# Three-block sequence model on one core: the first modulation tiles issued from POOL's queue, row tiles split over two pools, output scaled in pairs

## The chip, the cores and the metric

The kernel runs on one core of a Trainium2 chip. The metric is the device time of one execution in microseconds; three runs of a kernel are taken and their median is compared.

## What is computed

Three transformer-like blocks are applied to x of 256 tokens by 2048 channels, in float32. Cut to what matters here:

```python
c_act = jax.nn.silu(c)                                # c: 1 x 2048
mod = c_act @ w_ada[l] + b_ada[l]                     # 2048 x 12288
shift1, scale1, gate1, shift2, scale2, gate2 = jnp.split(mod, 6, axis=-1)
h = rms_norm(x, norm1) * (1.0 + scale1[:, None]) + shift1[:, None]
proj = h @ w_in                                       # block 1: gated delta rule, stick-breaking
...
x = second_block(x, mem_2, ...)                       # km, vm = projections of normed mem
return third_block(x, ..., final_norm_g_3)            # ends with rms_norm(x, final gain)
```

## The kernel before

x lies transposed: 16 tiles `x_k` of 128 channels by 256 tokens. Weights arrive as float32 tiles of 128x2048 (1 MiB each). Most matmuls split both operands: ScalarE writes a rounded high half (`whi`, `a` from line 390) and DVE the rest (`wlo` line 291, `a` line 391), and TensorE adds hi·hi, hi·lo and lo·hi. Every engine and queue runs its instructions in one fixed order, which a scheduler sets when the program is built; an instruction waits for semaphores, and what stands behind it waits too.

The head of the program is `block1` (line 516 on):

- `ada_start` loads c, applies SiLU and spreads it over the partitions (`csilu`). `ada_queue` then holds the 96 modulation tiles of w_ada, of which the first 32 give shift1 and scale1.
- `ada_tile` (line 489) loads one such tile, and DVE multiplies it by `csilu` and sums each row into a column of `mod` (line 496, 128x2048), then adds b_ada (line 498). The first 32 take their buffer from the pool `early`, tag "ada", three buffers; later ones share the weight pool's tag "wraw", three buffers (`WRAW`). All loads are issued by SyncE (SP).
- `load_mem` and `memory_kv` scale two tiles of mem into 16 `mh` tiles (line 951) and make four `km` tiles (matmuls at line 970, norm from line 972 on) and four `vm` tiles (line 990) for block 2; `load_x` is called before the fourth km, and modulation tiles are called for in between. The results go to DRAM (`kv_spill`).
- `project_rows` (line 593) takes 16 row tiles `wrow` of w_in's rows, one per k, from `early`, tag "rows", three buffers. For each k DVE scales x_k (line 611), ScalarE adds the shift (line 612), x_k is split, half of the row tile is split (`whi`, `wlo`), and 8 plain and 24 split matmuls run (line 623; the trace shows a plain one twice).
- The heads of block 1 follow, and then the other blocks, with weights from "wraw".

The tail: the last down-projection adds into `x[n]` for n = 0 to 15, squares go into `ssq`, `rstd_rows` makes the token scale, and `store_x` (line 467) writes x·gain·rstd with 16 DVE operations (line 472) and 16 stores of 128 KB (line 475).

Of the kernel before, what the change touches and what calls it, by code (L numbers as in the profile page):

```python
# [9 lines left out]
F32 = mybir.dt.float32  # L10
# [3 lines left out]
AF = mybir.ActivationFunctionType  # L14
ALU = mybir.AluOpType
# [3 lines left out]
P = 128  # L19
T = 256  # L20
D = 2048
KT = D // P
NFF = 5632 // P
GFF = 11
WRAW = 3
ADA_LATE = 6
NSPLIT = 8
X_AT = 3
SPILL_K = 7
# [175 lines left out]
class Core:  # L205
# [259 lines left out]
            self.square_acc(self.ssq, self.x[k], k == 0)  # L465

    def store_x(self, final=True):
        r = self.rstd_rows(self.ssq) if final else None
        for k in range(KT):
            if final:  # L470
                o = self.gt()
                self.nc.vector.scalar_tensor_tensor(o, self.x[k], self.vec("final", k), r, op0=ALU.mult, op1=ALU.mult)
            else:
                o = self.x[k]
            self.nc.sync.dma_start(self.out[:, k], o)

    def ada_start(self):
        nc, ins = self.nc, self.ins
        self.cs = self.adap.tile([P, D], F32, name="csilu")
        row = self.early.tile([P, D], F32, name="crow", tag="ada", bufs=3)[0:1]  # L480
        nc.sync.dma_start(row, ins["c"])
        for j in range(4):
            p = self.psum(False)
            nc.tensor.matmul(p, self.ones[0:1], row[:, j * 512:j * 512 + 512], start=True, stop=True)
            nc.scalar.activation(self.cs[:, j * 512:j * 512 + 512], p, AF.Silu)
        self.mod = self.const.tile([P, 96], F32, name="mod")
        self.ada_queue = [j + 16 * (1 - b) for j in range(16) for b in range(2)] + list(range(32, 96))

    def ada_tile(self, n):
        nc = self.nc  # L490
        if n < 32:
            raw = self.early.tile([P, 2048], F32, name=self.uid("ada"), tag="ada", bufs=3)
        else:
            raw = self.wp.tile([P, 2048], F32, name=self.uid("ada"), tag="wraw", bufs=WRAW)
        nc.sync.dma_start(raw, self.ins["w_ada"][n])
        nc.vector.scalar_tensor_tensor(raw, raw, 1.0, self.cs, op0=ALU.mult, op1=ALU.mult, accum_out=self.mod[:, n:n + 1])  # L496
        if n < 32:
            nc.vector.tensor_add(self.mod[:, n:n + 1], self.mod[:, n:n + 1], self.vec("b_ada", n))
        elif n % 16 == 15:
            k = VCOL["b_ada"]  # L500
            nc.vector.tensor_add(self.mod[:, n - 15:n + 1], self.mod[:, n - 15:n + 1], self.vecs[:, k + n - 15:k + n + 1])
# [14 lines left out]
    def block1(self):  # L516
        nc, ins = self.nc, self.ins
        with self.tc.tile_pool(name="ada", bufs=1) as self.adap:
# [11 lines left out]
            with self.tc.tile_pool(name="b1", bufs=1) as bp:  # L530
                self.bp = bp
                mixed = self.block1_mix()
                self.ada_some(96, 16 + ADA_LATE)
                h2 = []
# [58 lines left out]
    def project_rows(self, rstd, spills):  # L593
        nc = self.nc
        accs = [self.psum(width=512) for _ in range(2)]
        for lane in "SAB":
            with self.on(lane):
                accs += [self.psum(False) for _ in range(2)]
        self.hs = []
        for k in range(KT):  # L600
            while len(self.ada_queue) > 64 + 2 * max(0, KT - 2 - k):
                self.ada_some(1)
            raw = self.early.tile([P, 2048], F32, name=self.uid("wrow"), tag="rows", bufs=3)
            nc.sync.dma_start(raw, self.ins["w1_rows"][k])
            if k == SPILL_K:
                for dst, src in spills:
                    nc.sync.dma_start(dst, src)
            g = self.tp.tile([P, 1], F32, name=self.uid("gk"), tag="gk")
            nc.vector.scalar_tensor_tensor(g, self.mod[:, 16 + k:17 + k], 1.0, self.vec("norm1", k), op0=ALU.add, op1=ALU.mult)
            h = self.x[k]  # L610
            nc.vector.scalar_tensor_tensor(h, h, g, rstd, op0=ALU.mult, op1=ALU.mult)
            nc.scalar.activation(h, h, AF.Identity, bias=self.mod[:, k:k + 1])
            self.hs.append(self.split(h))
            parts = [self.split_weights(raw, a, min(1024, NSPLIT * P - a)) for a in range(0, NSPLIT * P, 1024)]
            for j in range(len(ROWS)):
                cols = slice(j * P, j * P + P)
                if j < NSPLIT:
                    whi, wlo = (t[:, j % 8 * P:j % 8 * P + P] for t in parts[j // 8])
                    pairs = [(whi, m) for m in self.hs[k][:2]] + [(wlo, self.hs[k][0])]
                else:  # L620
                    pairs = [(raw[:, cols], h)]
                for i, (w, m) in enumerate(pairs):
                    nc.tensor.matmul(accs[j // 2][:, j % 2 * T:j % 2 * T + T], w, m,  # L623
                                     start=(k == 0 and j % 2 == 0 and i == 0),
                                     stop=(k == KT - 1 and j % 2 == 1 and i == len(pairs) - 1))
        self.stash = {}
        for j, key in enumerate(ROWS):
            if j % 2 == 0:
                pair = self.act_halves("row")
            t = pair[j % 2]  # L630
            src = accs[j // 2][:, j % 2 * T:j % 2 * T + T]
            nc.gpsimd.memset(t[:, 0:3], 0.0)
            if j % 2:
                nc.vector.tensor_copy(t[:, 3:T + 3], src)
            else:
                nc.scalar.copy(t[:, 3:T + 3], src)
            self.stash[key] = t
# [35 lines left out]
    def proj(self, name, j):  # L673
        self.ada_some(1, 16 + ADA_LATE)
        return self.ftile(self.ins[name][j], self.hs)
# [182 lines left out]
    def sb_head(self, h, ob):  # L858
        nc, ins, c = self.nc, self.ins, self.c
        if h % 2 == 0:  # L860
            accs = self.ttile([ins["w1_sv"][h // 2, j] for j in range(2)], self.hs)
            self.sv = []
            for t in range(2):
                v = self.tmp("sv", (P, T), bufs=4)
                nc.scalar.copy(v, accs[t][:, :T])
                self.sv.append(v)
            self.ada_some(2, 16 + ADA_LATE)
        accq = self.proj("w1_sq", h)
# [65 lines left out]
    def memory_kv(self, load_x=None):  # L934
        nc, ins = self.nc, self.ins
# [7 lines left out]

        ssq = self.gt()
        for half, raw in enumerate(self.mem):
            pool, tag, bufs = (self.early, "rows", 3) if load_x else (self.wp, "wraw", WRAW)
            sq = pool.tile([P, 2048], F32, name=self.uid("msq"), tag=tag, bufs=bufs)
            nc.scalar.activation(sq, raw, AF.Square)
            for j in range(8):
                h = held()  # L950
                nc.vector.tensor_scalar(h, raw[:, j * T:j * T + T], self.vec("mem_g", half * 8 + j), None, op0=ALU.mult)
                hs.append(h)
            for w in (1024, 512):
                nc.vector.tensor_add(sq[:, :w], sq[:, :w], sq[:, w:2 * w])
            if half:
                nc.vector.tensor_add(ssq, ssq, sq[:, :T])
                nc.vector.tensor_add(ssq, ssq, sq[:, T:2 * T])
            else:
                nc.vector.tensor_add(ssq, sq[:, :T], sq[:, T:2 * T])
# [3 lines left out]
        for h in range(4):  # L963
# [15 lines left out]
            r = self.gt()  # L979
# [533 lines left out]
    def block3(self):  # L1513
        nc, ins = self.nc, self.ins
        hs = [self.split(self.x[k], self.vec("norm1_3", k)) for k in range(KT)]
        rstd, rcol = self.rstd_rows(self.ssq), self.rstd_cols(self.ssq)
        mixed = [None] * 16
        with self.tc.tile_pool(name="b3", bufs=1) as bp:
            cp = bp
            self.block3_mix(bp, hs, rstd, rcol, mixed)  # L1520
            self.ssq = self.new_ssq()
            for n in range(KT):
                self.wadd(self.x[n], self.wtile(ins["w3_out"][n], mixed))
                self.square_acc(self.ssq, self.x[n], n == 0)
        hs = [self.split(self.x[k], self.vec("norm2_3", k)) for k in range(KT)]
        rstd = self.rstd_rows(self.ssq)
        self.ssq = self.new_ssq()
        for g in range(NFF // GFF):
            a = []
            for f in range(g * GFF, (g + 1) * GFF):  # L1530
                acc = self.wtile(ins["w3_gate"][f], hs)
                gt = self.wmul(self.gt(), acc, rstd)
                nc.scalar.activation(gt, gt, AF.Silu)
                acc = self.wtile(ins["w3_up"][f], hs)
                nc.vector.tensor_mul(gt, gt, rstd)
                nc.vector.tensor_mul(gt, gt, self.wsum(self.gt(), acc))
                a.append(self.split(gt))
            for n in range(KT):
                self.wadd(self.x[n], self.wtile(ins["w3_down"][g, n], a))
                if g == NFF // GFF - 1:  # L1540
                    self.square_acc(self.ssq, self.x[n], n == 0)

    def block3_mix(self, bp, hs, rstd, rcol, mixed):
        nc, ins, tp = self.nc, self.ins, self.tp
# [152 lines left out]
```

## Time and profile before

| what | value |
|---|---|
| median of three runs | 3597.47 us (3594.34 to 3597.59) |
| the profiled execution's own time | 3601.28 us |
| span of its profile | 3599.5 us |
| TensorE busy | 3514.4 us, 98% |
| DVE busy | 2662.4 us, 74% |
| ScalarE busy | 1814.2 us, 50% |
| mean DMA rate over the span | 195 GB/s |

Busy times are of one profiled execution, and times in the rows are microseconds from the start of its span. Idle time is named with what ended it. TensorE's weight loads are counted apart and overlap its matmuls.

### The profile page before, as it was taken

How to read it: one execution, taken by the hardware profiler on the slowest of the kernel's cores; microseconds unless marked ns; L12 is line 12 of the kernel's file. 1: busy time of each engine (PE TensorE's matmuls, PEld its weight loads, DVE VectorE, ACT ScalarE, POOL GpSimd, SP SyncE). 2: the span in 40 equal slices, each digit the busy share in tenths (PEclk: the TensorE clock that was granted, in tenths of full speed). 3: DMA queues.
4: the chain of work that ended last, by engine and by line, in shares of the span. 5: the costliest groups of instructions: out<-in, count | busy, mean ns of one | idle time of the engine just before them, and what ended most of it. 6: DMA issues, size and time to landing. Idle time of an engine off the chain costs nothing.

```text
span 3599.5 us, 59008 instructions
## 1 busy us (share of the span) xinstructions
PE 3514.4 (98%) x22656; PEld 3144.6 (87%) x22656; DVE 2662.4 (74%) x5500; ACT 1814.2 (50%) x3138; POOL 61.6 (2%) x190
## 2 busy tenths in 40 slices
PE   8889999999999999999999999999999999999998
PEld 6889998999999998888888888889888888888887
DVE  7788988776767668877878867778776666666666
ACT  4156665544545455555555545554444544444444
POOL 0000000000000000000000000000000000000000
PEclk9989999999999999999999999999999999999999
DMA  8965777656666557332234336574445545555554
GB/s 337 351 237 200 263 266 265 225 208 219 222 206 231 188 181 239 133 125 107 103 115 138 125 117 213 188 253 170 172 168 185 187 176 202 176 198 180 195 184 144
DMA packets 128011, 700.99 MB, mean 195 GB/s; under 512 B 14449, under 2 KB 39537, under 8 KB 58865
## 3 DMA queue, kind: packets, MB, share of 16 engines
q1 hardware_dynamic: 127730, 697.22, 55.0%
q8 instruction: 179, 2.93, 0.3%
q14 instruction: 102, 0.84, 0.1%
HBM read 686.94 MB, written 10.22 MB: 194 GB/s over the span
## 4 chain that ended last, share of the span: by engine, by line
PE 86%; DVE 8%; ACT 3%; DMA 1%; issue 1%; SPq 0%; ACTq 0%; DVEq 0%
PE acc L335 36%; PE acc L339 18%; PE acc L309 12%; PE acc L313 6%; DVE wlo L291 2%; DVE ada L496 2%; PE acc L1349 1%; ACT whi L290 1%; PE acc L1358 1%; PE acc L1359 1%; PE acc L623 1%; PE acc L990 1%; PE acc L374 1%; DMA ada<-in_w_ada 1%; PE acc L369 1%
## 5 line engine op out<-in xcount | busy, mean ns | idle before, releaser
L290 ACT CAST whi<-wraw 128x1024 fp32r<-128x1024 f32 x1118 | 1096.1, 982 | 1199.0 <-PE acc L335 706.9
L291 DVE TENSOR_TENSOR wlo<-wraw,whi 128x1024 fp32r<-128x1024 f32 x1118 | 1272.7, 1140 | 514.5 <-ACT whi L290 412.4
L335 PE MATMUL acc<-a,whi 128*128 128x512 f32 x5888 | 1535.6, 396 | 6.7 <-ACT gt L346 1.7
L335 PEld LDWEIGHTS acc<-a,whi 128*128 128x128 f32 x5888 | 1043.1, 188 | 197.9 <-issue 5.4
L339 PEld LDWEIGHTS acc<-a,wlo 128*128 128x128 f32 x5888 | 816.9, 188 | 75.4 <-issue 4.0
L339 PE MATMUL acc<-a,wlo 128*128 128x256 f32 x5888 | 848.7, 282 | 0.0
L309 PE MATMUL acc<-a,whi 128*128 128x258 f32 (+1 forms) x3872 | 523.5, 284 | 0.2 <-ACT whi L290 0.2
L309 PEld LDWEIGHTS acc<-a,whi 128*128 128x128 f32 x3872 | 485.4, 190 | 0.9 <-ACT whi L290 0.4
L313 PE MATMUL acc<-a,wlo 128*128 128x258 f32 (+1 forms) x1936 | 282.8, 284 | 0.0
L313 PEld LDWEIGHTS acc<-a,wlo 128*128 128x128 f32 x1936 | 252.2, 190 | 0.3 <-issue 0.3
L496 DVE SCALAR_TENSOR_TENSOR ada<-ada,csilu 128x2048 f32<-128x2048 f32 x96 | 219.4, 2285 | 9.0 <-DMA ada<-in_w_ada 8.7
L1339 DVE COPY_PREDICATED ylo<-m_lev,acc 128x128 f32<-128x128 uint8 x200 | 82.8, 416 | 48.6 <-PE acc L1359 47.6
L369 PE MATMUL acc<-whi,a 128*128 128x256 f32 x416 | 108.3, 290 | 1.8 <-ACT whi L290 1.8
L1351 ACT COPY z<-yup 128x128 f32<-128x128 f32 x192 | 56.1, 300 | 102.5 <-DVE yup L1339 59.9
L370 PE MATMUL acc<-whi,a 128*128 128x256 f32 x416 | 107.6, 288 | 0.0
L356 DVE TENSOR_TENSOR x<-acc,x 128x256 f32<-128x256 f32 x128 | 54.2, 424 | 51.7 <-PE acc L339 51.7
L347 DVE TENSOR_TENSOR gt<-acc,gt 128x256 f32<-128x256 f32 x214 | 89.0, 418 | 3.5 <-ACT gt L346 2.9
L346 ACT COPY gt<-acc 128x256 f32<-128x256 f32 x214 | 78.0, 364 | 17.6 <-PE acc L339 17.6
L369 PEld LDWEIGHTS acc<-whi,a 128*128 128x128 f32 x416 | 80.0, 192 | 2.8 <-ACT whi L290 2.0
L370 PEld LDWEIGHTS acc<-whi,a 128*128 128x128 f32 x416 | 79.9, 192 | 0.0
L1359 PE MATMUL acc<-z,t 128*128 128x128 f32 x384 | 72.4, 278 | 0.2 <-ACT t L1352 0.2
L1358 PE MATMUL acc<-t,z 128*128 128x128 f32 x336 | 69.2, 290 | 2.0 <-ACT t L1352 2.0
(514 smaller groups left out, 3372.7 us busy)
## 6 DMA issues: line engine op xcount, KB each, us to landing
wraw<-in_w_up SPq DMA_DIRECT2D x132, 1024.0 KB, 4.8
ada<-in_w_ada SPq DMA_DIRECT2D x96, 1024.0 KB, 5.2
wraw<-in_w_down SPq DMA_DIRECT2D x128, 704.0 KB, 4.1
wraw<-in_w_out SPq DMA_DIRECT2D x48, 1024.0 KB, 4.9
wraw<-in_w_mg SPq DMA_DIRECT2D x48, 1024.0 KB, 4.9
wraw<-in_w_gate SPq DMA_DIRECT2D x44, 1024.0 KB, 4.7
wraw<-in_w_rs SPq DMA_DIRECT2D x20, 1024.0 KB, 5.1
wrow<-in_w_rows SPq DMA_DIRECT2D x16, 1024.0 KB, 8.5
```

Of the source, the lines that this page charges most:

```text
L290: nc.scalar.copy(hi[:, :m], raw[:, a:a + m])
L291: nc.vector.tensor_sub(lo[:, :m], raw[:, a:a + m], hi[:, :m].bitcast(F32))
L309: nc.tensor.matmul(acc, w, m, start=(n == 0), stop=False)
L313: nc.tensor.matmul(acc, lo[:, k % 8 * P:k % 8 * P + P], hs[k - c * kt][0], start=False, stop=(n == last))
L335: nc.tensor.matmul(both, hi[:, k % 8 * P:k % 8 * P + P], hs[k - c * kt][2], start=(n == 0), stop=False)
L339: nc.tensor.matmul(acc[:, :T], lo[:, k % 8 * P:k % 8 * P + P], hs[k - c * kt][0], start=False, stop=(n == last))
L347: self.nc.vector.tensor_add(out, acc[0], out)
L369: self.nc.tensor.matmul(accs[t], hs[k][0][:, ts], hi[:, ws], start=(k == 0), stop=False)
L370: self.nc.tensor.matmul(accs[t], hs[k][1][:, ts], hi[:, ws], start=False, stop=False)
L496: nc.vector.scalar_tensor_tensor(raw, raw, 1.0, self.cs, op0=ALU.mult, op1=ALU.mult, accum_out=self.mod[:, n:n + 1])
L1358: nc.tensor.matmul(pu4[:, 0, h], z2[:, h], t1[:, h], start=True, stop=True)
L1359: nc.tensor.matmul(pu4[:, 1, h], t1[:, h], z2[:, h], start=True, stop=True)
```

## The change

Three parts. The first 32 modulation tiles are issued from POOL's (GpSimd's) queue and have five buffers in `early` where they had three. The row tiles with odd k take their buffers from "wraw" of the weight pool; those with even k keep "rows", which has two buffers where it had three (the two squares of mem use that tag too). At the end ScalarE multiplies each finished `x[n]` by its gain into half of a pair tile, and after the token scale DVE multiplies a pair in place and SyncE stores it: 8 operations of 512 elements per partition and 8 stores of 256 KB.

```diff
+ADA_BUFS = 5
+ROW_BUFS = 2
...
     def store_x(self, final=True):
-        r = self.rstd_rows(self.ssq) if final else None
-        for k in range(KT):
-            if final:
-                o = self.gt()
-                self.nc.vector.scalar_tensor_tensor(o, self.x[k], self.vec("final", k), r, op0=ALU.mult, op1=ALU.mult)
-            else:
-                o = self.x[k]
-            self.nc.sync.dma_start(self.out[:, k], o)
...
+        r = self.rstd_rows(self.ssq).unsqueeze(1).to_broadcast([P, 2, T])
+        for j, y in enumerate(self.scaled):
+            self.nc.vector.tensor_mul(y, y, r)
+            self.nc.sync.dma_start(self.out[:, 2 * j:2 * j + 2], y)
+
+    def scale_x(self, n):
+        if n == 0:
+            self.scaled = []
+        if n % 2 == 0:
+            t = self.act.tile([P, 2, T + 4], F32, name=self.uid("fin"), tag="a")
+            self.scaled.append(t[:, :, :T])
+        self.nc.scalar.activation(self.scaled[-1][:, n % 2], self.x[n], AF.Copy, scale=self.vec("final", n))
...
-            raw = self.early.tile([P, 2048], F32, name=self.uid("ada"), tag="ada", bufs=3)
+            raw = self.early.tile([P, 2048], F32, name=self.uid("ada"), tag="ada", bufs=ADA_BUFS)
         else:
             raw = self.wp.tile([P, 2048], F32, name=self.uid("ada"), tag="wraw", bufs=WRAW)
-        nc.sync.dma_start(raw, self.ins["w_ada"][n])
+        (nc.gpsimd if n < 32 else nc.sync).dma_start(raw, self.ins["w_ada"][n])
...
-            raw = self.early.tile([P, 2048], F32, name=self.uid("wrow"), tag="rows", bufs=3)
+            if k % 2:
+                raw = self.wp.tile([P, 2048], F32, name=self.uid("wrow"), tag="wraw", bufs=WRAW)
+            else:
+                raw = self.early.tile([P, 2048], F32, name=self.uid("wrow"), tag="rows", bufs=ROW_BUFS)
...
-            pool, tag, bufs = (self.early, "rows", 3) if load_x else (self.wp, "wraw", WRAW)
+            pool, tag, bufs = (self.early, "rows", ROW_BUFS) if load_x else (self.wp, "wraw", WRAW)
...
                 if g == NFF // GFF - 1:
                     self.square_acc(self.ssq, self.x[n], n == 0)
+                    self.scale_x(n)
```

The scheduler orders the head anew with this; the engines' orders are the same behind it up to the tail. Two places follow. The first is DVE where row 0 begins: `x_301` is x0, `a_551` its lo half, `wlo_555` the lo half of row 0's weights, `ada_...` the modulation tiles and `mod` their sums. Before:

```order
107 L496 SCALAR_TENSOR_TENSOR ada_477,mod<-ada_477,csilu 128x2048
108 L498 TENSOR_TENSOR mod<-mod,vecs 128x1
109 L609 SCALAR_TENSOR_TENSOR gk_780<-mod,vecs 128x1
110 L611 SCALAR_TENSOR_TENSOR x_306<-x_306,gk_780,rstd_530 128x256
111 L496 SCALAR_TENSOR_TENSOR ada_499,mod<-ada_499,csilu 128x2048
112 L242 CAST m_lev<-mraw_523 128x896
113 L498 TENSOR_TENSOR mod<-mod,vecs 128x1
114 L391 TENSOR_TENSOR a_551<-x_301,a_551 128x256
```

And after the change, where line 506 is what line 496 was, line 393 what 391 was, and line 624 what 611 was:

```order
121 L506 SCALAR_TENSOR_TENSOR ada_990,mod<-ada_990,csilu 128x2048
122 L402 SCALAR_TENSOR_TENSOR rs_531<-rs_531,ms_528 128x256
123 L508 TENSOR_TENSOR mod<-mod,vecs 128x1
124 L506 SCALAR_TENSOR_TENSOR ada_994,mod<-ada_994,csilu 128x2048
125 L403 SCALAR_TENSOR_TENSOR rstd_530<-rs_531,rstd_530 128x256
126 L508 TENSOR_TENSOR mod<-mod,vecs 128x1
127 L506 SCALAR_TENSOR_TENSOR ada_1043,mod<-ada_1043,csilu 128x2048
128 L624 SCALAR_TENSOR_TENSOR x_301<-x_301,gk_547,rstd_530 128x256
...
135 L393 TENSOR_TENSOR a_551<-x_301,a_551 128x256
```

`ada_499` was the twelfth modulation tile on DVE, and the twelfth was the last before `a_551`. Now `ada_1043`, the twenty-third, stands there, and x0's scaling itself stands behind it.

The second place is SyncE's queue around the first row loads: `wrow_545` is row 0, `wrow_590` row 1, `wrow_635` row 2 and so on, `wraw` from w_vm a vm tile. Before:

```order
41 L931 DMA wraw_497<-in_w_vm 128x2048
42 L495 DMA ada_499<-in_w_ada 128x2048
43 L241 DMA mraw_523<-in_consts 128x896
44 L604 DMA wrow_545<-in_w_rows 128x2048
45 L604 DMA wrow_590<-in_w_rows 128x2048
46 L604 DMA wrow_635<-in_w_rows 128x2048
47 L495 DMA ada_770<-in_w_ada 128x2048
48 L604 DMA wrow_680<-in_w_rows 128x2048
49 L495 DMA ada_774<-in_w_ada 128x2048
50 L604 DMA wrow_725<-in_w_rows 128x2048
```

And after the change, a little later in the same queue:

```order
37 L243 DMA mraw_523<-in_consts 128x896
38 L620 DMA kv_spill<-mh_466 128x256
39 L617 DMA wrow_590<-in_w_rows 128x2048
40 L617 DMA wrow_680<-in_w_rows 128x2048
41 L620 DMA kv_spill<-mh_519 128x256
42 L617 DMA wrow_778<-in_w_rows 128x2048
43 L620 DMA kv_spill<-mh_283 128x256
44 L620 DMA kv_spill<-mh_519 128x256
45 L617 DMA wrow_725<-in_w_rows 128x2048
46 L548 DMA x_301<-in_x 128x256
47 L617 DMA wrow_884<-in_w_rows 128x2048
48 L548 DMA x_302<-in_x 128x256
```

No modulation tile stands among the row loads any more; the stores of km and vm and the reloads of x (which the output projection of block 1 adds to) stand there instead. Rows 0 and 2 have moved ahead of the last three vm tiles.

## Rows read from the trace of the kernel before

**Rows 1.** The page, part 1: busy time, share and instructions of each engine.
```profile
PE 3514.4 (98%) x22656; PEld 3144.6 (87%) x22656; DVE 2662.4 (74%) x5500; ACT 1814.2 (50%) x3138; POOL 61.6 (2%) x190
```

**Rows 2.** By stage: PE, PEld, DVE, ACT, POOL busy, PEclk, DMA share, GB/s.
```profile
10.00:20.00 10.00, 8.80 (x19) 5.48 (x18) 9.65 (x20) 6.00 (x6) 0.00 (x0) 1.00 1.01 426
8.90:83.50 74.60, 66.53 (x266) 54.03 (x265) 61.08 (x131) 37.57 (x59) 0.40 (x6) 0.95 0.87 342
83.50:136.90 53.40, 53.20 (x333) 48.92 (x331) 33.75 (x47) 13.16 (x22) 0.65 (x10) 1.00 0.87 327
136.90:205.90 69.00, 57.10 (x323) 50.84 (x323) 52.46 (x76) 18.55 (x32) 0.00 (x0) 0.93 0.87 348
...
3590.50:3598.50 8.00, 0.00 (x0) 0.00 (x0) 5.72 (x13) 0.00 (x0) 0.00 (x0) 0.50 0.78 259
```

**Rows 3.** Waits of SyncE's queue from 84 to 206 us: total, times, longest.
```profile
SPq L495 <- DVE mod L498: 45.2, 11, 5.8
SPq L604 <- PE acc L623: 27.6, 6, 5.4
```

**Rows 4.** Instructions of DVE by line, 0 to 206 us: busy, mean ns, idle before.
```profile
L496 DVE SCALAR_TENSOR_TENSOR ada<-ada,csilu 128x2048 f32<-128x2048 f32 x33 | 75.4, 2286 | 6.3 <-DMA ada<-in_w_ada 6.1
L291 DVE TENSOR_TENSOR wlo<-wrow,whi 128x1024 fp32r<-128x1024 f32 x16 | 19.3, 1224 | 14.5 <-ACT whi L290 14.5
```

**Rows 5.** Timeline of TensorE over the rows: start, duration, idle time before.
```profile
86.02 1.46 PE L623 MATMUL acc<-x,wrow 128*128 128x256 f32 x6
...
95.60 3.62 PE L623 MATMUL acc<-x,wrow 128*128 128x256 f32 x16
...
101.89 3.62 PE L623 MATMUL acc<-x,wrow 128*128 128x256 f32 x16
...
157.90 1.22 PE L623 MATMUL acc<-a,whi 128*128 128x256 f32 x8 [2.18 <-ACT whi L290]
...
166.60 1.21 PE L623 MATMUL acc<-a,whi 128*128 128x256 f32 x8 [2.15 <-ACT whi L290]
...
202.24 3.61 PE L623 MATMUL acc<-x,wrow 128*128 128x256 f32 x16
```

**Rows 6.** The chain that ended last, one late row: start, duration, what.
```profile
153.03 0.49 DVE x L611
153.51 2.22 DVE ada L496 x2
...
155.95 0.52 ACT x L612
...
156.80 1.05 ACT whi L290
...
157.88 1.23 DVE wlo L291
```

**Rows 7.** Timeline of DVE: 512 columns, two modulation tiles, the first lo half.
```profile
13.34 0.69 DVE L954 TENSOR_TENSOR msq<-msq 128x512 f32<-128x512 f32 x1
13.94 0.35 DVE L951 TENSOR_SCALAR mh<-wraw,vecs 128x256 f32<-128x256 f32 x1
...
73.00 2.28 DVE L496 SCALAR_TENSOR_TENSOR ada<-ada,csilu 128x2048 f32<-128x2048 f32 x1
...
75.40 2.28 DVE L496 SCALAR_TENSOR_TENSOR ada<-ada,csilu 128x2048 f32<-128x2048 f32 x1
...
83.56 1.77 DVE L391 TENSOR_TENSOR a<-x,a 128x256 fp32r<-128x256 f32 x5 [0.89 <-ACT a L390]
```

**Rows 8.** Timeline of all engines in the tail.
```profile
3583.36 0.42 ACT L429 ACTIVATE sq<-x 128x256 f32<-128x256 f32 x1 [3.40 <-DVE x L357]
3583.79 1.28 ACT L406 ACT_TABLE_LOAD   x1
...
3585.48 0.42 ACT L406 ACTIVATE rstd<-ms 128x256 f32<-128x256 f32 x1 [0.41 <-DVE ms L440]
...
3589.04 7.27 DVE L472 SCALAR_TENSOR_TENSOR gt<-x,vecs,rstd 128x256 f32<-128x256 f32 x16
```

More of the change, by code (lines that the diff above doesn't have):

```diff
@@ L467, in store_x @@
     def store_x(self, final=True):
-        r = self.rstd_rows(self.ssq) if final else None
-        for k in range(KT):
-            if final:
-                o = self.gt()
-                self.nc.vector.scalar_tensor_tensor(o, self.x[k], self.vec("final", k), r, op0=ALU.mult, op1=ALU.mult)
-            else:
-                o = self.x[k]
-            self.nc.sync.dma_start(self.out[:, k], o)
+        if not final:
+            for k in range(KT):
+                self.nc.sync.dma_start(self.out[:, k], self.x[k])
+            return
+        r = self.rstd_rows(self.ssq).unsqueeze(1).to_broadcast([P, 2, T])
[9 more added lines that the diff above has]
+        self.nc.scalar.activation(self.scaled[-1][:, n % 2], self.x[n], AF.Copy, scale=self.vec("final", n))
     def ada_start(self):
@@ L479, in ada_start @@
         self.cs = self.adap.tile([P, D], F32, name="csilu")
-        row = self.early.tile([P, D], F32, name="crow", tag="ada", bufs=3)[0:1]
+        row = self.early.tile([P, D], F32, name="crow", tag="ada", bufs=ADA_BUFS)[0:1]
         nc.sync.dma_start(row, ins["c"])
```

## The prediction

> **What bounds the kernel now.** I read the page's busy shares first, then the head by stages, then the waits and the chain inside it, and last the tail. TensorE is busy for 98% of the span [rows 1], so time can only be won where it stands idle. The change moves instructions at two places alone: before block 1's first head, and after the last down-projection. The stages of the head [rows 2] show three resources close together. Up to 83.5 us DVE is busy 61.08 of 74.60 us and the DMA engines 0.87; from 83.5 to 136.9 TensorE is busy throughout (53.20 of 53.40); from 136.9 to 205.9 it works only 57.10 of 69.00. Two rates come from the same group: 426 GB/s at a DMA share of 1.01 is what full DMA engines carry, 342 is the mean up to 83.5 us.
>
> The matmuls of `project_rows` start at 86.02 us [rows 5] and end at 202.24 + 3.61 = 205.85 us: 119.8 us for 16 rows. A row that waits for nothing takes 101.89 − 95.60 = 6.29 us, so 16 of them would take 100.6 us; later rows take 166.60 − 157.90 = 8.70 us, with 2.18 us of idle TensorE in each. The chain [rows 6] says why: a late row is two modulation tiles on DVE (2.22 us each), the scaling of x (0.49), ScalarE's bias (0.52) and whi (1.05), and DVE's wlo (1.23), one behind the other. SyncE's queue stands behind the same DVE: 45.2 us of its waits in this stretch are a modulation tile's buffer that DVE has not read, 27.6 are row buffers [rows 3]. So 19.2 us are lost in the rows, to modulation tiles that are consumed between them.
>
> **The modulation tiles.** Their number stays 32; what changes is where DVE meets them. In DVE's order 12 stand before the first lo half of x (`a_551`) in the kernel before, and 23 after. Three wlo of rows also move ahead of it (with the first, which stood behind). TensorE works in order, and row 0 needs x0. So:
>
> 1. *The rows start later.* DVE begins `a_551` at 83.56 us [rows 7]. Eleven tiles more: one takes 2.29 us [rows 4] and repeats every 75.40 − 73.00 = 2.40 us [rows 7], so 26.4 us. Three wlo of 1.22 us [rows 4]: 3.7 us. With the work there already, DVE has 61.1 + 26.4 + 3.7 = 91.2 us to do from 8.9 us on; without any wait it is done at 100.1 us, with as much waiting as before (74.6 − 61.1 = 13.5) at 113.6 us.
> 2. *The loads bound the same moment.* By then 23 modulation tiles, two of mem, eight of km and vm and three rows must have landed, 36 of 1 MiB, with 2 MiB of x, the level table of 0.44 MiB and about 1 MiB of spills, some 39.5 MiB or 41.4 MB. At 426 GB/s that is 97 us; the first tile of it, 1.05 MB or 2.5 us, has landed when DVE starts at 8.9 us, so loading starts at about 6.4 us and could end at 104 us. At 342 GB/s it is 121 us, and the end 127 us. Five buffers beside the row buffers should keep the engines fuller than three did, but tiles that DVE does not yet need are loaded too. The rate needed for 113.6 us is 41.4 MB in 107.2 us, 386 GB/s, between the two. I take 113.6 us, bounds 104 and 127.
> 3. *The rows then run at TensorE's pace.* DVE has nine tiles left (21.6 us), 13 wlo (15.9) and per row about 1 us of scaling and lo: under 60 us in 100. The loads left are 13 rows and 9 tiles, 22 MiB or 23 MB, which is 54 us at 426 GB/s. Both hide behind 100.6 us of matmuls. If that cover goes (rows arriving late through two `rows` buffers), a row costs up to 2.2 us more, as now. TensorE stood idle before them; its granted clock in stretches with such gaps is 0.93 and 0.95 instead of 1.00 [rows 2], and I allow 1.0 us for a slow first row. The rows end at 113.6 + 100.6 + 1.0 = 215.2 us, **9.3 us later** than 205.85; with the bounds of step 2, from −0.2 to +22.8 us.
>
> **The row buffers.** Half of the rows now share the three buffers that km, vm and later weights use, and x is reloaded between rows on SyncE. A reload waits until its row's matmuls have read x, and what stands behind it waits too. Row 7's load stands behind the reload of x0, row 6's behind x1's: three to four rows of lead, 19 us or more at 6.29, against some 5 us for a load. I count nothing. In return, reloads and row loads are out of the way when the heads start; nothing before shows this gain. I bound it by 0 and by TensorE's idle time in the last stretch of rows, 69.0 − 57.1 = 11.9, and take 1.0, since the weights behind that stretch were released late by the same tiles.
>
> **The tail.** ScalarE gains 16 scalings of 128x256 (0.42 us each by the Ln [rows 8]) beside TensorE's last matmuls; 15 are hidden, since it is idle for 3.40 us before the last square [rows 8]. The last one moves the table load that starts at 3583.79 by 0.42 us; it ends at 3585.49, when the Ln began anyway (3585.48). DVE's 16 operations of 7.27 us become 8 of 512 elements at 0.60 to 0.69 [rows 7], about 5.2: at most 2.4 us less. But 2.10 MB still leave the chip, at 259 GB/s with the engines 0.78 busy [rows 2]: 8.1 us before, 6.3 if they were 1.0 busy. Lines stay 1 KB in SBUF. I take 0.8, bounds 0 and 2.4.
>
> **The sum.** +9.3 − 1.0 − 0.8 = **+7.5 us**. The profiled execution took 3601.28 us (span 3599.5) and would take 3608.8; the median of the runs shown is 3.81 us below it, so the median becomes 3597.47 + 7.5 = **3605.0 us**. The bound of 0.2% is 7.2 us, about what a measurement of this kernel can tell from no change.
>
> **A rule weighed.** SyncE's queue spends 45.2 us of the rows waiting at modulation tiles [rows 3], so a second queue takes more than issue time from it. The Trainium skill (DMA: Bandwidth & Descriptors, "Issuing engines are not separate DMA queues") holds that DMAs started by different engines run on the same 16 DMA engines, and that starting them on several saves only the sequencer's time. The DMA share of 1.01 with one queue agrees that nothing is left above 426 GB/s; by that rule step 2's bound of 104 us stands, and the gain of the second queue is only that nothing waits behind a full buffer. The same page ("Queues, rings and completion order") says the engines take turns between queues that have work; by it mem, km and vm would land late while POOL's queue is full, which no row of one queue can show.
>
> **Rivals.**
> - *A. Nothing to measure (0.22).* DVE waits less than before and the loads reach 104 to 109 us. The rows end between 205.6 and 210.6; the total is within ±3 of now, about 3598 us. For it: 426 GB/s in the early window. Against: kv and x loads with short lines, and 0.87 over the whole stretch.
> - *B. Faster (0.18).* Here the gain is behind the rows. If loading keeps 426 GB/s, the rows start at 104 us and end level; every load of the head is then done before the heads' weights are due, and half or more of the 11.9 us of idle TensorE that the old head leaves does not come back as a new wait there. With the tail at 2.4 that gives −8 to −10, about 3589 us. It decides when the rows start before 106 us and their step stays under 6.4 us.
> - *C. Much slower (0.16).* POOL's queue delivers no better than the mean of 342 GB/s, since km and vm wait behind 1 MiB tiles that DVE cannot use yet, and DVE waits for TensorE's km products in its order: rows from 127 us, +22.8 − 1.8 = +21, about 3618 us. For it: the three kinds of loads are needed by one in-order DVE, and its waits before are mostly for loads.
> - *D. The change does not do what it says:* POOL's issues stand in the order of the kernel, so I give this nothing of its own.
>
> **How the numbers follow.** The forecast (start of rows at 109 to 120 us, +3 to +14) has 0.44. Slower by over 7.2 us: rather more than half of it, 0.25, and C: 0.41. Within 7.2 us: the rest of it, 0.19, and A: 0.41. Faster: B, 0.18. The forecast's own range is 3600 to 3611. The range for 8 in 10 takes in A and most of B, and of C the part below its price: 3588 to 3616 us, with about 0.06 left out below and 0.12 above.
>
> **What would show it.** Right: the first matmul of the rows at 110 to 118 us instead of 86, TensorE idle 20 us or more before it; rows 6.3 us apart to the end, with no idle time for whi; 23 modulation tiles on DVE before the first `a`; a DMA share over 0.9 up to then; the output's DVE time about 5 us with the last store leaving at most 2.4 us earlier against the last x. Wrong: rows that start before 106 us or after 122, rows that still take 8.7 us, or rows that end near 215 us while the heads behind them take another time than now. Were the sum right and the rest of the middle different by more than 2 us, the moved loads would have changed later stages, which I count as unchanged.

## The result and the profile after

The changed kernel takes 3622.39 us (median of four runs, 3618.6 to 3623.0) against 3597.17 us before: a ratio of 1.0067, 95% interval 1.0055 to 1.0079, **25.2 us slower**. The forecast was +7.5 us, its range ended at 3616, and rival C stood at +21.

The page of the changed kernel, parts 1 and 3 (busy time; DMA queue, kind: packets, MB, share of 16 engines):

```profile
PE 3509.4 (97%) x22656; PEld 3142.8 (87%) x22656; DVE 2651.0 (73%) x5492; ACT 1819.7 (50%) x3154; POOL 75.0 (2%) x222
...
q1 hardware_dynamic: 122994, 663.66, 52.3%
q0 software_dynamic: 4608, 33.56, 2.4%
```

q0 is POOL's queue: 32 tiles of 1 MiB. By stage, with the columns of [rows 2], where the fourth stretch ends at the first row's matmul:

```profile
8.90:83.50 74.60, 43.98 (x156) 33.30 (x157) 45.84 (x96) 24.28 (x33) 6.86 (x13) 0.86 0.93 374
83.50:136.90 53.40, 36.72 (x160) 31.69 (x159) 45.57 (x85) 19.83 (x37) 6.33 (x12) 0.84 0.95 369
136.90:205.90 69.00, 69.00 (x440) 64.46 (x440) 37.72 (x62) 18.42 (x32) 2.15 (x19) 1.00 0.67 239
...
8.90:129.10 120.20, 72.96 (x280) 57.85 (x280) 83.61 (x162) 39.57 (x59) 12.66 (x24) 0.87 0.95 377
```

The DMA engines are fuller than before (0.93 and 0.95 instead of 0.87), and yet TensorE and DVE do less up to 83.5 us: 43.98 instead of 66.53 and 45.84 instead of 61.08. TensorE's timeline in the changed kernel shows where the time is (start, duration, idle time before):

```profile
24.31 12.98 PE L983 MATMUL acc<-mh,wraw 128*128 128x256 f32 x48 [8.10 <-DMA wraw<-in_w_km]
...
75.53 1.22 PE L989 MATMUL acc<-sq,c_ones 128*128 128x256 f32 x2 [19.53 <-ACT sq L987]
...
129.16 1.22 PE L636 MATMUL acc<-x,wrow 128*128 128x256 f32 x2 [12.50 <-ACT x L625]
...
132.23 0.63 PE L636 MATMUL acc<-a,whi 128*128 128x256 f32 x2
...
222.84 3.62 PE L636 MATMUL acc<-x,wrow 128*128 128x256 f32 x16
...
229.12 3.62 PE L636 MATMUL acc<-x,wrow 128*128 128x256 f32 x16
232.38 2.23 PE L311 MATMUL acc<-a,whi 128*128 128x256 f32 x16
```

The rows start at 129.16 us (86.02 before), 43.1 later; they then follow 6.28 us apart (229.12 − 222.84) and the heads begin at 232.38 (205.50 before), so the rows give 16.3 us back. The waits of DVE from 0 to 130 us, and ScalarE's timeline where the longest of them comes from:

```profile
DVE rs L401 <- ACT gt L409: 17.8, 1, 17.8
DVE mh L964 <- DMA wraw<-in_mem: 13.1, 2, 10.3
DVE m_lev L244 <- DMA mraw<-in_consts: 5.7, 1, 5.7
```

```profile
49.29 0.42 ACT L409 ACTIVATE gt<-gt 128x256 f32<-128x256 f32 x1
69.74 1.04 ACT L292 CAST whi<-wrow 128x1024 fp32r<-128x1024 f32 x1 [20.03 <-DMA wrow<-in_w_rows]
70.80 1.28 ACT L408 ACT_TABLE_LOAD   x1
```

ScalarE's order holds the cast of row 0's weights ahead of the second km's norm (`gt`). It stands there for 20.03 us until row 0 has landed, the km chain stands behind it, and DVE stands behind the chain, with 12 modulation tiles done by 83.5 us, no more than before. The chain that ended last, in the same stretch, runs through SyncE's loads (start, duration, what):

```profile
24.88 15.46 DMA x<-in_x
...
40.35 17.35 DMA x<-in_x
...
57.72 11.99 DMA wrow<-in_w_rows
```

The 16 loads of x on SyncE's queue land later, in the view of the DMA issues (KB each, median us from issue to landing) of the kernel before up to 86 us, and then of the changed kernel from 8.9 to 129.1 us:

```profile
x<-in_x SPq DMA_DIRECT2D x16, 128.0 KB, 3.3
```

```profile
x<-in_x SPq DMA_DIRECT2D x16, 128.0 KB, 16.8
```

At the end of the program the forecast's tail came out: DVE's eight operations take 4.90 us instead of 7.27 [rows 8]. The last scaling moves the table load by about 0.4 us, and the load still ends (3606.93 + 1.28 = 3608.21) when the Ln behind it can begin (3608.23), as the prediction had said.

```profile
3606.10 0.42 ACT L431 ACTIVATE sq<-x 128x256 f32<-128x256 f32 x1 [3.02 <-DVE x L359]
3606.42 0.49 ACT L485 ACTIVATE fin<-x,vecs 128x256 f32<-128x256 f32 x1
...
3606.93 1.28 ACT L408 ACT_TABLE_LOAD   x1
...
3608.23 0.42 ACT L408 ACTIVATE rstd<-ms 128x256 f32<-128x256 f32 x1
...
3611.78 4.90 DVE L476 TENSOR_TENSOR fin<-fin,rstd 128x512 f32<-128x512 f32 x8
3612.50 4.97 SPq L477 DMA_DIRECT2D out_x<-fin  x8
```

### The profile page after: what moved, and what is told of

It is laid out like the page before. It is cut to its first block, busy times and chain, and to the rows that moved or that the text cites. A ratio compares the mean times of both kernels' runs of the same rounds, so it can differ in the third digit from the quotient of the medians.

```text
span 3620.9 us, 59012 instructions
## 1 busy us (share of the span) xinstructions
PE 3509.4 (97%) x22656; PEld 3142.8 (87%) x22656; DVE 2651.0 (73%) x5492; ACT 1819.7 (50%) x3154; POOL 75.0 (2%) x222
## 4 chain that ended last, share of the span: by engine, by line
PE 86%; DVE 7%; DMA 3%; ACT 2%; issue 1%; SPq 0%; DVEq 0%; ACTq 0%
PE acc L337 36%; PE acc L341 18%; PE acc L311 11%; PE acc L315 6%; PE acc L636 3%; DVE wlo L293 2%; PE acc L1362 1%; PE acc L1371 1%; PE acc L1372 1%; DVE ada L506 1%; DMA x<-in_x 1%; ACT whi L292 1%; PE acc L376 1%; PE acc L371 1%; PE acc L372 1%
## 5 line engine op out<-in xcount | busy, mean ns | idle before, releaser
L348 ACT COPY gt<-acc 128x256 f32<-128x256 f32 x214 | 78.2, 365 | 18.6 <-PE acc L341 18.5
```

## The experiments

The theory (S): a queue of their own lets 23 modulation tiles stand ahead of row 0 in DVE's order, and its transfers share the DMA engines with what SyncE loads for km, x and row 0, so that these land late and the engines wait in their fixed orders. The rivals are named in the expectations.

**One part alone, four times.** First, the kernel before with only the queue changed:

```diff
-        nc.sync.dma_start(raw, self.ins["w_ada"][n])
+        (nc.gpsimd if n < 32 else nc.sync).dma_start(raw, self.ins["w_ada"][n])
```

> The kernel before with one edit: the first 32 modulation tiles are issued from POOL's queue (three buffers, rows and tail as before). Theory S (the second queue): a queue of their own lets 24 modulation tiles stand ahead of row 0's lo half on DVE, and shares the DMA engines with SyncE's loads, so mem, x and row 0 land late; the rows' first matmul comes at 118 to 132 us (before 86.0, after 129.2), 16 rows take 101 to 104 us, and the total is +17 to +27 us. Rival R1 (the row buffers: odd rows in the weight pool, two buffers for even ones) expects no change here, within 3 us. Rival R2 (five buffers: POOL runs far ahead and starves SyncE) expects a third to a half of the +25 at most.

Measured: 3635.34 us, ratio 1.0102 (1.0087 to 1.0117), 37 us slower, worse than the whole change and above every expectation. The rows start at 133.2 us, and ScalarE stands at row 0's load for 17.3 us in the same place. R1 and R2 fall: the queue, together with the new order that the scheduler makes of it, does it without the other parts, and the whole change, with five buffers, split rows and the new tail, is 12 us better. How much of the 37 us is the order is asked below.

Then the row buffers alone:

```diff
-            raw = self.early.tile([P, 2048], F32, name=self.uid("wrow"), tag="rows", bufs=3)
+            if k % 2:
+                raw = self.wp.tile([P, 2048], F32, name=self.uid("wrow"), tag="wraw", bufs=WRAW)
+            else:
+                raw = self.early.tile([P, 2048], F32, name=self.uid("wrow"), tag="rows", bufs=2)
```

> The kernel before with one edit: odd row tiles take buffers of the weight pool, even ones keep two. Theory S: 12 modulation tiles stay ahead of row 0, start of the rows at 84 to 88 us, total within 4 us of before. R1: the rows or km and vm wait for each other's buffers, +10 us or more, up to +25. R2: no change.

Measured: 3599.81 against 3598.39, ratio 1.0005 (0.9995 to 1.0014). The rows end at 197.5 us, 8.0 earlier than before, but the first addition of block 1's output projection comes at 597.6 instead of 600.7: 4.9 us of the gain are given back in the heads, which take 400.1 us instead of 395.2.

The whole change with its tiles on SyncE again:

```diff
-        (nc.gpsimd if n < 32 else nc.sync).dma_start(raw, self.ins["w_ada"][n])
+        nc.sync.dma_start(raw, self.ins["w_ada"][n])
```

> The changed kernel with its modulation tiles issued from SyncE again (five buffers, split rows and the paired tail stay). Theory S: 12 tiles ahead of row 0 as before; rows start at 82 to 88 us, total between -5 and +3 us against before, of which the tail gives about -1.3. R1: slower by 10 us or more. R2: five buffers let modulation tiles run ahead in one queue too, so km, vm and rows come later: +5 to +15.

Measured: 3599.1, ratio 1.0 (0.999 to 1.001). Rows from 84.6 to 200.9 us. As S expected: without the second queue nothing is lost, and nothing that can be measured is won; R1 and R2 fall here too.

The tail alone, as in the change's diff of `store_x` and `scale_x`:

> The kernel before with only the tail changed (ScalarE scales x, DVE multiplies pairs, eight stores). From the last x to the end of the span the kernel before took 16.66 us and the changed one 15.32: all theories expect 15.0 to 15.6 us there and a total of -1.3 us (between -2.4 and 0), too little for the timed rounds to tell from none.

Measured: 3598.92, ratio 1.0002 (0.9993 to 1.0011), no difference to be told. From the start of the last `ssq` addition to the end of the span it is 14.3 us (3585.19 to 3599.5), 14.35 in the changed kernel (3606.55 to 3620.9), 15.7 before (3583.81 to 3599.5).

**The wait at row 0's weights.** The buffers of even and odd rows were swapped, which puts the cast of row 0 behind three km norms:

```diff
-            if k % 2:
+            if k % 2 == 0:
```

> The changed kernel with the two kinds of row buffers swapped: even row tiles from the weight pool, odd ones from early. In ScalarE's order the cast of row 0's weights then stands behind the norms of the first three km instead of ahead of the second; 23 modulation tiles stay ahead of row 0 on DVE. Theory S1 (ScalarE stands in its order at row 0's load, 20.0 us, DVE behind it 17.8 us): that wait goes, rows start at 112 to 122 us instead of 129.2, total +8 to +18 us against before. Rival R4 (the DMA engines' bytes set the moment, the wait hides under them): rows start at 126 to 130 us, total +22 to +27.

Measured: 3634.85, ratio 1.0104 (1.0089 to 1.0119), slower than the changed kernel; rows from 131.1 us. S1 falls in the form in which I had put it: the wait went, and others took its place. By stage up to 83.5 us, then TensorE's timeline, then waits of ScalarE and DVE from 0 to 140 us in this kernel:

```profile
8.90:83.50 74.60, 46.13 (x164) 34.71 (x164) 60.27 (x121) 25.60 (x37) 9.54 (x18) 0.90 1.02 416
```

```profile
72.15 5.14 PE L1003 MATMUL acc<-wraw,mh 128*128 128x256 f32 x16 [11.40 <-DMA wraw<-in_w_vm]
88.86 20.44 PE L1003 MATMUL acc<-wraw,mh 128*128 128x256 f32 x86 [11.57 <-DMA wraw<-in_w_vm]
```

```profile
ACT mh L1007 <- PE acc L1003: 28.3, 2, 25.7
...
DVE ssq L432 <- ACT sq L431: 19.4, 1, 19.4
```

Now the DMA engines are full (1.02, 416 GB/s) and DVE has 17 tiles done by 83.5 us instead of 12, but the bytes are tiles: vm lands late, TensorE stands 23 us for it, ScalarE behind TensorE, DVE behind ScalarE.

**Order without the second queue.** The kernel before, with eleven more tiles called for ahead of row 0:

```diff
         for k in range(KT):
+            if k == 0:
+                self.ada_some(11)
             while len(self.ada_queue) > 64 + 2 * max(0, KT - 2 - k):
```

> The kernel before with one edit: eleven more modulation tiles are called for ahead of row 0, all on SyncE's queue with three buffers. 23 tiles then stand on DVE ahead of row 0's wlo, as in the changed kernel, but no second queue shares the DMA engines with mem, x and row 0. The forecast's own step (order alone): the split matmuls of row 0 start at 108 to 118 us, rows then 6.3 us apart, total +4 to +12. Rival R5 (order alone gives all of it): start at 125 us or later, total +18 to +27. Rival R6 (order alone costs nothing): within 3 us of before.

Measured: 3620.53, ratio 1.0067 (1.0051 to 1.0084), +22.3, which is past the forecast's +4 to +12 and inside R5's +18 to +27. The timeline of TensorE, that of SyncE's queue (start, duration with the waits between the issues), and the stage up to the rows:

```profile
114.97 1.22 PE L625 MATMUL acc<-x,wrow 128*128 128x256 f32 x2 [30.07 <-DMA wrow<-in_w_rows]
```

```profile
74.68 32.98 SPq L495 DMA_DIRECT2D ada<-in_w_ada  x11
107.72 1.59 SPq L606 DMA_DIRECT2D wrow<-in_w_rows  x3
```

```profile
8.90:114.90 106.00, 67.32 (x277) 54.78 (x275) 92.75 (x182) 44.67 (x75) 0.92 (x14) 0.85 0.90 348
```

The start is 115.0 us, inside the expected 108 to 118, so R5's mechanism (125 or later) falls though its total came. R6 falls. Two limits meet at this start: row 0's load is issued only at 107.7 us, behind the eleven tiles in SyncE's queue, and lands as TensorE starts; DVE, with its 23 tiles, comes to row 0's wlo at 116.5. The rows end at 218.3, 12.8 later than before; the profiled span is 18.5 longer, of which about 3 us arise between 613 and 1454 us and 3 behind that; their cause stays open.

So the order alone, with the start where the forecast had it, costs three times the forecast's +7.5. With the same old buffers and both, order and second queue, it was +37 (the queue alone, above): some 22 us are the order, some 15 come with the second queue. Order alone with the new buffers was not run.

**First tiles on SyncE, later ones on POOL.** The changed kernel with a count:

```diff
+        self.ada_no = getattr(self, "ada_no", 0) + 1
-        (nc.gpsimd if n < 32 else nc.sync).dma_start(raw, self.ins["w_ada"][n])
+        (nc.gpsimd if 12 < self.ada_no <= 32 else nc.sync).dma_start(raw, self.ins["w_ada"][n])
```

> The changed kernel with its first 12 modulation tiles on SyncE's queue and the other 20 on POOL's; DVE's order keeps 12 tiles ahead of row 0. Theory S: the head is as before up to row 0 (start of the rows at 82 to 90 us); the later tiles do not wait behind row loads; total between -12 and +2 us against before. Rival R3 (POOL's transfers are slow by themselves): the rows wait for modulation tiles and the total is +5 us or more.

Measured: **3590.87, ratio 0.9978 (0.9969 to 0.9987), 7.4 us faster than the kernel before and 31.5 than the changed one.** R3 falls. By stage and by SyncE's waits from 84 to 230 us in this kernel:

```profile
8.90:83.50 74.60, 66.48 (x267) 54.20 (x266) 61.00 (x132) 37.82 (x60) 2.77 (x5) 0.95 0.95 377
83.50:136.90 53.40, 49.95 (x304) 45.86 (x303) 38.91 (x55) 13.11 (x21) 5.28 (x10) 0.97 1.02 416
136.90:205.90 69.00, 64.96 (x408) 59.79 (x407) 51.66 (x95) 28.39 (x51) 4.96 (x28) 0.98 0.76 292
```

```profile
SPq L618 <- PE acc L637: 40.9, 8, 7.9
```

The first stage is that of the kernel before. From 83.5 to 136.9 us the DMA engines are full, and none of the first 32 modulation tiles waits for its buffer on SyncE any more (45.2 us before, [rows 3]); what its queue waits for now is row buffers: the rows run from 85.8 to 197.8 us and end 7.7 earlier than before. The whole change without the second queue had won nothing (+0.7, above), so with these buffers the queue is worth some 8 us.

With nine on SyncE:

> The changed kernel with its first nine modulation tiles on SyncE and 23 on POOL; 14 tiles stand ahead of row 0 on DVE (12 with twelve on SyncE, 23 in the changed kernel). Theory S: two tiles more are 5 us of DVE ahead of row 0, and x and vm share the engines earlier: rows start at 88 to 98 us, total between -6 and +6 against before, not better than the run with twelve on SyncE (-7.4). Rival (the more tiles early the better, as long as DVE has idle time): -9 or less.

Measured: 3593.07 against 3598.44, ratio 0.9987 (0.9977 to 0.9996), −5.4; rows from 85.3 to 199.2. The rival's −9 does not come: two more tiles early win nothing over twelve on SyncE, and the 2 us between the two runs are within their intervals.

With five, where 23 tiles stand ahead of row 0 again:

> The changed kernel with its first five modulation tiles on SyncE and the other 27 on POOL. DVE keeps 23 tiles ahead of row 0's lo half of x, as in the changed kernel, but mem and the first three km no longer share the DMA engines with a second queue. Theory S (the late start is 23 tiles, 115 us as in the run with the tiles first on one queue, and the rest, 14 us, is SyncE's loads arriving late beside POOL's): start of the rows at 112 to 122 us, total +8 to +18. Rival R7 (the early loads do not matter; 23 tiles with their DVE and ScalarE order set 129 us): start at 126 to 132, total +21 to +28.

Measured: 3621.05, ratio 1.0059 (1.0044 to 1.0074), four runs from 3614.43 to 3622.66. TensorE and the stage up to the rows:

```profile
13.83 9.19 PE L984 MATMUL acc<-mh,wraw 128*128 128x256 f32 x28 [0.71 <-DMA wraw<-in_w_km]
...
116.54 1.22 PE L637 MATMUL acc<-x,wrow 128*128 128x256 f32 x2 [14.88 <-ACT x L626]
```

```profile
8.90:116.50 107.60, 70.93 (x277) 56.38 (x276) 85.69 (x162) 38.77 (x58) 12.28 (x23) 0.87 1.01 411
```

The start is S's, 12.6 us before the changed kernel's; R7 falls for the start. The total, +22.6, is R7's and not S's: the rows end 12.7 us earlier than in the changed kernel, the first output addition of block 1 comes 9.2 us earlier (613.2 against 622.4), and the profiled span is the same (3620.9). Where those 9 us go behind 613 us stays open; TensorE's busy time in stages of 300 us differs by 3 us at most. So an earlier start of the rows is not shown to be an equal gain in the total.

Twelve on SyncE, but with the old buffers (three for tiles, three for rows) and the new tail:

> The kernel before with the first 12 modulation tiles on SyncE, the other 20 on POOL, and the new tail; three buffers each for tiles and rows as before. If the second queue alone gives the gain of the run with twelve on SyncE (-7.4): -5 to -10. If the five buffers and the split rows carry it: within 3 us of before.

Measured: 3608.94, ratio 1.0029 (1.0018 to 1.0041), 10.5 us slower than before; outside both expectations. The order ahead of row 0 is that of the kernel before, but SyncE's queue waits longer for row buffers and ScalarE for rows (waits of SyncE from 84 to 230 us, and of ScalarE from 0 to 140; 25.3 in the run with five buffers):

```profile
SPq L613 <- PE acc L632: 56.5, 11, 8.6
```

```profile
ACT whi L290 <- DMA wrow<-in_w_rows: 34.4, 7, 6.9
```

So the split rows and five buffers, which do nothing without the queue, decide whether the second queue gains or loses here. Which of the two does it was not tried.

**Turns by packet.** In the changed kernel's view of the DMA engines, 9 to 24 us, where both queues carry lines of 8 KB (a line is what a transfer moves into one partition), and then 36 to 56 us, where SyncE carries x with lines of 1 KB (packets, MB, share):

```profile
q1 hardware_dynamic: 438, 3.20, 50.8%
q0 software_dynamic: 434, 3.16, 50.2%
```

```profile
q0 software_dynamic: 833, 6.05, 73.9%
q1 hardware_dynamic: 1308, 2.12, 28.1%
...
x<-in_x SPq DMA_DIRECT2D x8, 128.0 KB, 16.7
```

Equal lines share equally; with short lines SyncE's queue carries 2.12 of 8.17 MB. The turns are not strictly packet for packet, though: 1308 packets of SyncE's queue went beside 833 of POOL's. To test it the modulation tiles were loaded in pieces of 512 columns, 2 KB for each partition, first all 96 of them:

```diff
-        (nc.gpsimd if n < 32 else nc.sync).dma_start(raw, self.ins["w_ada"][n])
+        for q in range(0, 2048, 512):
+            (nc.gpsimd if n < 32 else nc.sync).dma_start(raw[:, q:q + 512], self.ins["w_ada"][n][:, q:q + 512])
```

> The changed kernel with each modulation tile loaded by four transfers of 512 columns, so with lines of 2 KB instead of 8 KB; all orders stay. Theory P (with both queues at work the DMA engines take turns by packet, so that x's lines of 1 KB lose to POOL's of 8 KB): x lands in 6 to 12 us instead of 16.8, row 0's load earlier, rows start 5 to 15 us before 129.2, total +10 to +20. Rival: turns go by something else; x lands in 15 to 18 us, total +23 to +28, or later if shorter lines cost rate.

Measured: 3630.03, ratio 1.009 (1.0074 to 1.0105). The rows start at 121.9 us, 7.2 earlier, and x lands in 13.7 us (median) instead of 16.8: the direction of P, less than it asked for. But block 1's heads took 406 us (from 224.9 to 631.0) instead of 390 (232.4 to 622.4), where the later tiles, also in four pieces, stand on SyncE. So once more, with POOL's 32 tiles alone in pieces:

> The changed kernel with the 32 tiles of POOL's queue loaded by four transfers of 512 columns each (lines of 2 KB), all else as in the changed kernel; the later 64 tiles keep their one transfer, which the earlier run with short lines did not. Theory P (turns by packet): rows start at 118 to 126 us as in that run (121.9), and without its loss in the heads the total is +14 to +21. If the loss in the heads comes from POOL's short lines, the total is +27 or more again.

Measured: 3616.21 against 3598.44, ratio 1.005 (1.0035 to 1.0065), +17.8, as P expected. Rows from 121.4 to 224.3 us, heads 393 us. The loss of the earlier run was SyncE's pieces. Pieces on the competing queue give back 8 us of the start.

That the packets' length does it is not shown, since the pieces change more than that. The view of the DMA engines from 36 to 56 us, and POOL's waits from 0 to 140 us in this kernel and then in the changed one:

```profile
DMA packets 3197, 7.68 MB, mean 384 GB/s; under 512 B 504, under 2 KB 1788, under 8 KB 3054
...
q0 software_dynamic: 1585, 5.19, 68.9%
```

```profile
POOL ada L507 <- DMA ada<-in_w_ada: 51.0, 57, 2.3
```

```profile
POOL ada L505 <- DVE ada L506: 103.1, 23, 20.7
```

The 5.19 MB of the tiles went in 3054 − 1788 = 1266 packets between 2 and 8 KB, 4.1 KB each, so the packets are half as long as before and not a quarter. And POOL now issues a piece when an earlier one has landed, where it had waited for DVE to free a whole tile: it begins with eight pieces (2 MiB) at once instead of four tiles (4 MiB), and from 9 to 24 us its queue carries 2.40 MB instead of 3.16. That rival for the earlier landing of km, mem and x was not tested.

## Why the prediction was wrong

*What bounds the kernel, and where the tiles go.* Right. 23 tiles stood ahead of row 0, the rows then ran 6.28 us apart to the end without a wait for whi, and the 16 rows took 103.2 us (129.16 to 232.38), 1.6 over the forecast: the first row's pairs of matmuls took 0.63 us instead of 0.40.

*Step 1, the term that failed:* "with as much waiting as before (74.6 − 61.1 = 13.5) at 113.6 us". The start came at 129.2, past the step's upper bound of 127 too. DVE's work up to the rows was 83.6 us, less than the 91.2 of the sum, but its waiting was 120.2 − 83.6 = 36.6 us instead of 13.5. Of these 36.6, 17.8 are ScalarE at row 0's load, 8.1 are mem behind 8.9 us, 5.7 the level table, and the rest short waits for TensorE and ScalarE. With 23 tiles ahead on one queue the sum for the start holds: 92.75 us of work, 106.0 − 92.75 = 13.3 of waiting, rows from 115.0. So the failed step is the waiting, which I carried over from a kernel with one queue; what a second queue does to it was left out of the forecast and given to rival C. In the changed kernel's profile it is the whole miss: the start came 15.6 us after the forecast's and the span 13.9 above it.

*What the right start would not have mended.* The way from the start to the total does not hold either. Order alone started its rows at 115.0 and cost +22.3, and five tiles on SyncE started them at 116.5 and cost +22.6, where the forecast made +7.5 of 113.6. In the first of them the rows end 3.1 us after the forecast's 215.2, and another 6 us arise behind the heads, which the prediction counted as unchanged; their cause stays open. The last 3.8 lie between its profile and the medians.

*Step 2, the loads.* How fast 41.4 MB arrive was the wrong question. 377 GB/s from 8.9 to 129.1 us is close to the 386 I had assumed. What counted was whose bytes they were: by 129 us POOL's queue had carried 27.74 MB and SyncE's 19.78, in which mem, x, row 0 and the level table came late. The order of landing, not the sum of bytes, set the waits, and in the run with the swapped buffers full engines at 416 GB/s gave a still later start.

*The row buffers.* "I count nothing" holds for the change of buffers alone (1.4 us, not to be told from none). The gain behind the rows was 5.2 us (the heads up to the first output addition took 390.0 instead of 395.2), where I took 1.0. Which part of the change gives it was not isolated: with the row buffers alone the heads took 400.1.

*The tail.* 1.3 us where I took 0.8, inside its bounds. The gain is real in the profile and too small for the runs.

*The sum in measured terms:* +43.1 for the start, −16.3 for the rows, −5.2 in the heads, −1.3 in the tail, +1.1 elsewhere, in all +21.4 between the two profiled spans (3599.5 and 3620.9). The medians differ by 3.8 more; the profiled execution of the kernel before was one of its slower ones, as the prediction noted.

*The rivals.* C had the place (km and vm behind tiles that DVE cannot use yet, rows from 127 us) and nearly the price (+21). Its reason was partly wrong: POOL's queue did not deliver at 342 GB/s, the engines were fuller than before. DVE did wait for the km products in its order, but by way of ScalarE, which stood at row 0's load. A and B did not happen: the rows did not start before 109 us.

*The rule.* That a second queue gains only issue time (the Trainium skill, DMA: Bandwidth & Descriptors, "Issuing engines are not separate DMA queues") is not borne out: with the first twelve tiles on SyncE it took the 45.2 us of waiting for tile buffers out of SyncE's queue and made the kernel 7.4 us faster, though with the old buffers the same queues lost 10.5. That the engines take turns between queues (the same page of the Trainium skill, "Queues, rings and completion order") agrees with the equal shares at 9 to 24 us; its turns by packet agree in direction with 74% against 28% where lines differ, but the profile's packets did not alternate one for one (833 and 1308).

## What to carry to other kernels

A load moved to a second queue got no bandwidth of its own here: it took it from the loads of the first queue, and most from those with short lines. So try the second queue with those transfers alone that are needed after what the first queue is loading, and measure it with the buffers it will have: the same 20 tiles gained 7.4 us with one set of buffers and lost 10.5 with another. When a queue moves, read the new fixed order on every engine for an instruction that waits for a late load ahead of work that could go on, and count that wait anew instead of carrying over the old kernel's. Price a head by which load each engine waits for next, not by the sum of bytes at a mean rate. And do not carry a changed start straight into the total: two runs that began their rows where the forecast had them were still 22 us slower.

## What was not expected of the hardware

- Two queues with lines of 8 KB shared the DMA engines equally (3.20 and 3.16 MB in 15 us), while a queue that carried mostly x's lines of 1 KB got 2.12 of 8.17 MB; x took a median of 16.8 us to land instead of 3.3.
- Eight stores of 256 KB kept the DMA engines at 0.99 and 335 GB/s while they ran (3613.3 to 3619.4 us), where sixteen of 128 KB had 0.78 and 259 GB/s [rows 2], with lines of 1 KB in both.
- One transfer of 1 MiB by lines of 8 KB cost POOL about 0.5 us to issue (2.23 us for four); its queue stood 103.1 us of the first 140 waiting for DVE to free buffers, so POOL's issuing was no limit.
